# Strassen's seven block products for part of each second feed-forward matrix in a two-layer decoder trunk

## The chip, the cores and the metric

The kernel runs on one core of one Trainium2 chip. The metric is the device time of one execution in microseconds (us). Engines are named as in the profile: PE is TensorE (matmuls), PEld its weight loads, DVE is VectorE, ACT is ScalarE, POOL is GpSimd, SP is the engine whose queue starts the weight DMAs.

## The reference

The trunk works on 256 tokens of width 1024 and has two layers. Each layer is a feed-forward half step, a token mixer (a gated spatial unit and a differential attention side by side) and a second feed-forward half step, each followed by a layer norm over a scaled residual. There are four feed-forwards in all, and the change touches only them:

```python
def _swiglu(x, w1, w3, w2):
    return (jax.nn.silu(x @ w1) * (x @ w3)) @ w2
...
        h = _swiglu(x, ffn_w1[l, 0], ffn_w3[l, 0], ffn_w2[l, 0])
        x = _layernorm(ALPHA * x + 0.5 * h, ln_g[l, 0], ln_b[l, 0])
```

`w1` and `w3` are 1024 x 2816, `w2` is 2816 x 1024, all float32. The inner width 2816 is 22 k tiles of 128.

## The kernel before

**Number format.** Each float32 operand is split in two: a high part rounded to TensorE's fp32r type (ScalarE, a copy) and a low part, the difference (VectorE, a subtraction). A product is then three matmuls, high x high, low weight x high and high weight x low (`three`, matmuls at L208). For a weight piece of 1024 columns the high part is L166 and the low part L168, in `stream`; for activations they are L173 and L174, in `split`.

**Weights.** `stream` loads a piece of 1 MB (128 x 2048) into one of 4 `raw` buffers over SP's queue and splits it into two high and two low tiles of 1024 columns, out of 8 buffers each (`hi`, `lo`). A piece that is loaded early waits for these buffers, which come free when TensorE has used the tile. When the next stage's first weights would have to wait, some go to buffers of the activation pool instead (`lent`).

**A feed-forward** (`ffn`) has three parts. `gemm_b2` computes the first 4 of the 22 inner tiles with tokens as rows. Then `gemm_a2` runs nine times and makes two inner tiles each: 32 matmuls with the high weights over 512 columns (L220), 32 with the low weights over 256 columns (L227), an addition from PSUM (L230), silu on ScalarE (L523), a product on VectorE (L524) and the split of the result (L173, L174). Last comes the second matrix, in two calls of `gemm_b`, one for each 512 output columns: for each of 22 k tiles and each half of 128 tokens, three matmuls of 512 columns into one PSUM bank per token half. That is 264 matmuls (22 x 2 x 2 x 3) in a row. The last `tail` k tiles of a call are held back, so that token half 0 is finished ahead of token half 1: 4 k tiles in the first call, 14 in the second. In the last feed-forward of all, the block of token half 1 and column half 1 is computed in two banks of 256 columns.

`Norm.part` (L415, L419) adds a finished PSUM block to the scaled residual and takes its statistics, `Norm.finish` normalises a token half, `turned` transposes it on TensorE for the next stage.

**Order.** The order on TensorE is the order of the code. VectorE, ScalarE and the queues are ordered by a scheduler, from priorities that grow with each piece of weights (`step`). Each engine works its list strictly in that order. Pieces of work that are to lie beside the matmuls (`beside`, `beat`) are placed by counting matmul work.

Of the kernel before, what the change touches and what calls it, by code (L numbers as in the profile page):

```python
# [25 lines left out]
DFF = 2816  # L26
FT = DFF // P
FB = 4
HEADS = 8
HD = 64  # L30
GROUPS = 8
# [16 lines left out]


@with_exitstack  # L50
def trunk(ctx, tc, x, xT, w13a, w13b, w2, wb, wqk, wa, wbr, wo, gateb, sgug, sgub, sguwT, sgubias, lam, diffg,
          lng, lnb, lngT, lnbT, cosT, sinT, out):
    nc = tc.nc
    V, A, G, PE = nc.vector, nc.scalar, nc.gpsimd, nc.tensor
# [184 lines left out]
    def rows_b(ps, t, k0, piece, xh, xl, kts, c0=0, n=512):  # L239
# [6 lines left out]
                  k == 0, k == kts - 1)  # L246
        beat(n / 1024)

    def gemm_b(src, kts, xh, xl, done, tail=4, last=()):

        blocks = [[(bank(), c, n) for c, n in (last if t else ()) or ((0, 512),)] for t in range(NT)]
        held = []
        for c in range(0, kts, 4):
            nk = min(4, kts - c)
            for i, piece in enumerate(stream(src[:, c * 512 : (c + nk) * 512], nk * 512)):
                k = c + 2 * i
                if k >= kts - tail:
                    held.append((k, piece))
                    continue
                for t in range(NT):  # L260
                    for ps, o, n in blocks[t]:
                        rows_b(ps, t, k, piece, xh, xl, kts, o, n)
        for t in range(NT):
            for ps, o, n in blocks[t]:
                for k, piece in held:
                    rows_b(ps, t, k, piece, xh, xl, kts, o, n)
                done(t, ps[:, :n], o, n)

    def gemm_b2(srcs, xh, xl, done, norm=None):

# [115 lines left out]
    class Norm:  # L386
# [25 lines left out]
        def part(self, t, c, ps):  # L412
            s = slice(c, c + ps.shape[1])
            with behind(self.xlo.get((0, 0))):
                V.scalar_tensor_tensor(out=self.y[t][:, s], in0=self.y[t][:, s], scalar=self.scale, in1=ps,  # L415
                                       op0=ALU.mult, op1=ALU.add)
            for o in range(s.start, s.stop, self.group):
                g = o // self.group * 6
                V.bn_stats(out=self.st[t][:, g : g + 6], in_=self.y[t][:, o : o + self.group])  # L419
            if self.last and t == NT - 1 and s.stop < D:  # L420
                V.tensor_tensor(out=self.y[t][:, s], in0=self.y[t][:, s], in1=self.g[:, s], op=ALU.mult)
# [70 lines left out]

    def ffn(l, f, i, norm, last=False):
        xh, xl = parts(both)
        h_hi = [act.tile([P, 512], F32R, tag="slot", name=name("hhi")) for _ in range(FT // 2)]
        h_lo = [act.tile([P, 512], F32R, tag="slot", name=name("hlo")) for _ in range(FT // 2)]
        hh, hl = view(h_hi), view(h_lo)

        def front(t, ps):
            s = t512("silu")  # L500
# [4 lines left out]
        def turned(t, s):  # L505
            b = side_bank()
            for k in range(FB):
                PE.transpose(b[:, k * P : (k + 1) * P], s[:, k * P : (k + 1) * P], ident)  # L508
            b4 = b.rearrange("p (k t) -> p k t", k=4)
            for j in range(2):  # L510
                hi = h_hi[j].rearrange("p (k t) -> p k t", k=2)[:, :, t * P : (t + 1) * P]
                lo = h_lo[j].rearrange("p (k t) -> p k t", k=2)[:, :, t * P : (t + 1) * P]
                split(hi, lo, b4[:, 2 * j : 2 * j + 2])
            yield 0

# [4 lines left out]
        for j in range(FB, FT, 2):  # L520
            for m, z in gemm_a2([w13a[l, f, j - FB + m] for m in range(2)], both, lambda m: t512("silu")):
                s = z[:, :T]
                silu[0] = A.activation(s, s, AF.Silu).ins  # L523
                V.tensor_tensor(out=s, in0=s, in1=z[:, T:], op=ALU.mult)  # L524
                split(hh(j + m), hl(j + m), s)
# [5 lines left out]
        def done(t, p, c, n):  # L531
            ln.part(t, 512 + c, p)
            if c + n == 512:
                ln.finish(t, ((2, 1.5), (2, 1))[t])
# [227 lines left out]
    for l in range(DEPTH):  # L762
# [2 lines left out]
        norm = ffn(l, 1, 2, norm, last=l == DEPTH - 1)  # L765


_INS = ["x", "xT", "w13a", "w13b", "w2", "wb", "wqk", "wa", "wbr", "wo", "gateb", "sgug", "sgub", "sguwT", "sgubias",
        "lam", "diffg", "lng", "lnb", "lngT", "lnbT", "cosT", "sinT"]


def _layout(i):
# [34 lines left out]
    o["w2"] = halves(f["ffn_w2"])  # L807
# [40 lines left out]
```

## Time and profile before

| what | value |
|---|---|
| time, three runs | 1243.22, 1243.42 (median), 1244.21 us |
| span of the profiled execution | 1242.5 us, 0.9 us below the median of the runs; it has no other time of its own |
| TensorE busy | 1236.6 us (100% of the span) |
| VectorE busy | 873.1 us (70%) |
| ScalarE busy | 756.0 us (61%) |
| DMA | 241.87 MB, 195 GB/s in the mean |
| granted TensorE clock | 1.000 |

Busy shares are means over stages of different kinds. A row of a group gives the line, the engine, the operation, out<-in with the shape, the count, then the busy us with the mean ns of one, and the idle time just ahead of these instructions with what ended it. The first feed-forward's column groups run from 36 to 128.6 us, its second matrix to 188.5 us.

### The profile page before, as it was taken

What the parts mean: (1) busy time and instruction counts of PE and PEld (TensorE: products, weight loads), DVE (VectorE), ACT (ScalarE), POOL (GpSimd) and SP (SyncE); (2) the same over time, 40 slices, a digit from 0 to 9 for tenths busy, and PEclk for the clock granted to TensorE, in tenths of its full rate; (3) what the DMA queues carried; (4) which work ended last, traced back from release to release, by engine and by line L of the source; (5) the groups of instructions that cost most, each with busy time, mean ns of one, the idle gap of its engine ahead of it and who ended that gap; (6) DMA issues with size and microseconds to landing.
All of it is one profiled execution on the core that took longest, in us unless ns stands there. A gap on an engine that the chain in (4) does not pass through costs nothing.

```text
span 1242.5 us, 17870 instructions
## 1 busy us (share of the span) xinstructions
PE 1236.6 (100%) x6703; PEld 1064.1 (86%) x6703; DVE 873.1 (70%) x1532; ACT 756.0 (61%) x1388; POOL 86.0 (7%) x184
## 2 busy tenths in 40 slices
PE   9999999999999999999999999999999999999998
PEld 8888888888888888888888888888888888888887
DVE  6766567876587977665677665679756879766753
ACT  6776446679665566664466664466786555766640
POOL 0100000144100000000000000002430000000000
PEclk9999999999999999999999999999999999999999
DMA  9765645654754745556545546556556456455540
GB/s 352 276 204 183 224 171 187 227 167 165 248 183 145 244 162 205 177 180 253 194 169 191 192 159 250 203 184 206 162 175 228 165 174 233 170 203 203 165 174 35
DMA packets 40679, 241.87 MB, mean 195 GB/s; under 512 B 5344, under 2 KB 6416, under 8 KB 14480
## 3 DMA queue, kind: packets, MB, share of 16 engines
q1 hardware_dynamic: 36624, 227.82, 52.1%
q0 software_dynamic: 3536, 12.13, 3.0%
q8 instruction: 52, 0.85, 0.3%
q10 hardware_dynamic: 432, 0.79, 0.2%
q14 instruction: 35, 0.29, 0.1%
HBM read 235.47 MB, written 1.05 MB: 190 GB/s over the span
## 4 chain that ended last, share of the span: by engine, by line
PE 99%; DVE 0%; ACT 0%; issue 0%; DVEq 0%; ACTq 0%
PE bank L220 38%; PE bank L208 35%; PE bank L227 20%; PE bank L323 2%; PE sbank L588 1%; PE sbank L474 1%; PE sbank L637 1%; PE sbank L718 1%; PE sbank L335 0%; PE sbank L635 0%; PE sbank L659 0%; PE sbank L508 0%; PE sbank L622 0%; PE sbank L627 0%; PE sbank L446 0%; DVE xtok L454 0%
## 5 line engine op out<-in xcount | busy, mean ns | idle before, releaser
L168 DVE TENSOR_TENSOR wlo<-raw,whi 128x1024 fp32r<-128x1024 f32 (+1 forms) x442 | 490.0, 1127 | 223.4 <-PE bank L227 129.3
L166 ACT ACTIVATE whi<-raw 128x1024 fp32r<-128x1024 f32 (+1 forms) x442 | 425.8, 978 | 279.4 <-PE bank L208 135.3
L220 PE MATMUL bank<-x,whi 128*128 128x512 f32 x1792 | 426.5, 392 | 0.0
L220 PEld LDWEIGHTS bank<-x,whi 128*128 128x128 f32 x1792 | 330.7, 188 | 69.0 <-issue 2.6
L227 PE MATMUL bank<-x,wlo 128*128 128x256 f32 x1792 | 229.9, 284 | 0.0
L227 PEld LDWEIGHTS bank<-x,wlo 128*128 128x128 f32 x1792 | 224.2, 191 | 4.8
L208 PE MATMUL bank<-whi,hhi 128*128 128x512 f32 (+1 forms) x374 | 141.3, 378 | 0.0
L208 PE MATMUL bank<-wlo,hhi 128*128 128x512 f32 (+1 forms) x374 | 141.0, 377 | 0.0
L208 PE MATMUL bank<-whi,hlo 128*128 128x512 f32 (+1 forms) x374 | 140.9, 377 | 0.0
L228 ACT ACTIVATE r<-bank 128x256 f32<-128x256 f32 x256 | 96.5, 380 | 66.0 <-PE bank L227 65.7
L208 PE MATMUL bank<-whi,x 128*128 128x512 f32 x328 | 106.6, 394 | 0.0
L208 PEld LDWEIGHTS bank<-whi,hlo 128*128 128x128 f32 x374 | 70.4, 188 | 13.0
L208 PEld LDWEIGHTS bank<-wlo,hhi 128*128 128x128 f32 x374 | 70.4, 188 | 12.7
L208 PEld LDWEIGHTS bank<-whi,hhi 128*128 128x128 f32 x374 | 70.4, 188 | 12.7
L208 PEld LDWEIGHTS bank<-whi,x 128*128 128x128 f32 x328 | 61.6, 188 | 12.7
L208 PE MATMUL bank<-wlo,x 128*128 128x512 f32 x164 | 64.0, 390 | 0.0
L480 ACT ACTIVATE xf<-sbank,ln_b,ln_g 128x128 f32<-128x128 f32 x80 | 30.0, 456 | 40.2 <-PE sbank L474 40.2
L230 DVE TENSOR_TENSOR silu<-bank,r 128x256 f32<-128x256 f32 x144 | 54.2, 418 | 0.2
L383 POOL DMA_DIRECT2D bc<-in_lng x6 | 3.2, 530 | 727.7 <-DVE bc L382 727.7
L415 DVE SCALAR_TENSOR_TENSOR xtok<-xtok,bank 128x512 f32<-128x512 f32 (+1 forms) x25 | 16.6, 663 | 42.2 <-PE bank L208 42.2
L564 POOL TENSOR_TENSOR swap<-swap,sin_t 128x512 f32<-128x512 f32 x16 | 24.3, 1517 | 242.4 <-DMA swap<-z 226.7
L208 PE MATMUL bank<-lhi,x 128*128 128x512 f32 x120 | 39.9, 396 | 0.0
(183 smaller groups left out, 1254.1 us busy)
## 6 DMA issues: line engine op xcount, KB each, us to landing
raw<-in_w13a SPq DMA_DIRECT2D x72, 1024.0 KB, 5.0
raw<-in_w SPq DMA_DIRECT2D x40, 1024.0 KB, 4.9
raw<-in_wa SPq DMA_DIRECT2D x24, 1024.0 KB, 5.5
raw<-in_wb SPq DMA_DIRECT2D x16, 1024.0 KB, 4.9
raw<-in_wqk SPq DMA_DIRECT2D x16, 1024.0 KB, 5.1
raw<-in_wbr SPq DMA_DIRECT2D x16, 1024.0 KB, 4.9
raw<-in_w13b SPq DMA_DIRECT2D x12, 1024.0 KB, 5.0
raw<-in_wo SPq DMA_DIRECT2D x8, 1024.0 KB, 4.9
```

The source lines that it names most:

```text
L166: A.activation(h, r, AF.Copy)
L168: V.tensor_tensor(out=w, in0=r, in1=h.bitcast(F32), op=ALU.subtract)
L208: PE.matmul(ps, xx, w, start=start and n == 0, stop=stop and n == 2)
L220: PE.matmul(b[-1], hi[:, k * P : (k + 1) * P], xc(k), start=k == 0, stop=False)
L227: PE.matmul(b[n][:, :T], lo[:, k * P : (k + 1) * P], xc(k)[:, :T], start=False, stop=k == KT - 1)
L228: emptied[0] = A.activation(r[:, s], b[n][:, T:], AF.Copy, scale=scale).ins
L230: a = V.tensor_tensor(out=z[:, s], in0=b[n][:, :T], in1=r[:, s], op=ALU.add)
L323: PE.matmul(ps[t][m], x[:, j, o + t * P : o + (t + 1) * P], y, start=k0 + j == 0 and o == 0 and y is hi, stop=k0 + j == KT - 1 and y is lo)
L415: V.scalar_tensor_tensor(out=self.y[t][:, s], in0=self.y[t][:, s], scalar=self.scale, in1=ps, op0=ALU.mult, op1=ALU.add)
L474: PE.transpose(b[:, k * P : (k + 1) * P], self.y[t][:, h * 512 + k * P : h * 512 + (k + 1) * P], ident)
L480: A.activation(xf[:, s], b[:, s], AF.Identity, scale=self.gT[:, f], bias=self.bT[:, f])
L564: turned_by[0] = G.tensor_tensor(out=s3, in0=s3, in1=s, op=ALU.mult).ins
```

## The change

Of the 11 pairs of inner k tiles, six (`SQ`: tiles 4 and 5 up to 14 and 15) go through Strassen's seven products in the second matrix; five (`PQ`: 0 and 1, 2 and 3, 16 to 21) stay as they were. For a Strassen pair the 2 x 2 blocks are two token halves by two k tiles for the activations, and two k tiles by two column halves for the weights. The seven block products accumulate in seven PSUM banks `S[1]` to `S[7]`, over all six pairs.

- `mixed` makes the four sums of activation blocks on VectorE (L563 to L566) and splits the originals and the sums, 512 columns each (L177, L178), where two tiles of 256 were split.
- `stream_s` loads both column halves of a pair as one piece of 1 MB, splits three of the four blocks (`cut`, L294 on ScalarE and L296 on VectorE), makes three sums in place in `raw` on VectorE (L307, L309, L310) and splits the four results. Two pairs share one tile for their first block, so a pair takes three and a half tiles.
- After the sixth pair eight VectorE operations and one of ScalarE recombine the blocks into the residual (L464, L466, L622 to L626). `S[2]`, `S[3]` and `S[4]` stay open and become the sums of three of the four output blocks of the plain pairs.
- The plain pairs come last, with both column halves in one piece. The last four (`HELD`) are held back, so token half 0 ends 48 matmuls ahead of token half 1.
- The activation pool grows from 27 to 31 buffers; the ring of DMA descriptors that GpSimd writes is set to 8192 bytes.

The weights are only ordered otherwise in memory. Sums of weight blocks are made on the chip.

```diff
+NS = 6
+SQ = [(FB + 2 * p, FB + 2 * p + 1) for p in range(NS)]
+PQ = [(k, k + 1) for k in (0, 2, *range(FB + 2 * NS, FT, 2))]
+HELD = 4
...
-    act = ctx.enter_context(tc.tile_pool(name="act", bufs=27))
+    act = ctx.enter_context(tc.tile_pool(name="act", bufs=31))
...
+    def stream_s(src, pair):
+        step()
+        raw = raw_pool.tile([P, CH], F32, tag="raw", name=name("raw"))
+        nc.sync.dma_start(raw, src)
...
+        def cut(p, o, n):
+            h, w = (v[:, p[2] : p[2] + n] for v in p[:2])
+            r = raw[:, o : o + n]
+            with behind(latest[0]):
+                A.activation(h, r, AF.Copy)
+            with behind(latest[1]):
+                V.tensor_tensor(out=w, in0=r, in1=h.bitcast(F32), op=ALU.subtract)
...
+        b, c, d = ((*two(), 0) for _ in range(3))
+        cut(a, 0, 512)
+        cut(b, 1024, 1024)
+        V.tensor_tensor(out=raw[:, :1024], in0=raw[:, :1024], in1=raw[:, 512:1536], op=ALU.add)
+        cut(c, 0, 1024)
+        V.tensor_tensor(out=raw[:, 1024:1536], in0=raw[:, :512], in1=raw[:, 1024:1536], op=ALU.add)
+        V.tensor_tensor(out=raw[:, 1536:], in0=raw[:, 1024:1536], in1=raw[:, 1536:], op=ALU.add)
+        cut(d, 1024, 1024)
...
+        return keep, {1: at(a, 0), 3: at(b, 0), 2: at(b, 1), 5: at(c, 0), 7: at(c, 1), 6: at(d, 0), 4: at(d, 1)}
...
+        def mixed(q, qa):
+            qb = s512("qb")
+            a = qa.rearrange("p (k t) -> p k t", k=4)
+            V.tensor_tensor(out=qb[:, :T].rearrange("p (k t) -> p k t", k=2),
+                            in0=a[:, 1:2].to_broadcast([P, 2, P]), in1=a[:, ::3], op=ALU.subtract)
+            V.tensor_tensor(out=qb[:, T : T + P], in0=qb[:, P:T], in1=qa[:, :P], op=ALU.subtract)
+            V.tensor_tensor(out=qb[:, T + P :], in0=qa[:, T : T + P], in1=qb[:, T : T + P], op=ALU.add)
...
+            for j, v in enumerate((qa, qb)):
+                split(at[0][j], at[1][j], v)
...
-        gemm_b(w2[l, f, 0], FT, hh, hl, lambda t, p, c, n: ln.part(t, 0, p))
...
-        gemm_b(w2[l, f, 1], FT, hh, hl, done, tail=14, last=((0, 256), (256, 256)) if last else ())
+        S = {n: side_bank() for n in (3, 7, 4)}
+        S.update({n: bank() for n in (1, 2, 5, 6)})
+        pair = None
+        for n, q in enumerate(SQ):
+            pair, w = stream_s(w2s[l, f, n], pair)
+            for b in (3, 7, 4, 1, 2, 5, 6):
+                three(S[b], *s_op[q][b], *w[b], n == 0, n == NS - 1 and b in (1, 5, 6, 7))
+            beat(1.75)
+        u, v = s512("u"), s512("v")
+        A.activation(u, S[6], AF.Copy)
+        ln.more(1, 0, S[7], ALU.subtract, ln.scale)
+        ln.more(0, 0, S[1], ALU.add, ln.scale)
+        V.tensor_tensor(out=u, in0=u, in1=S[1], op=ALU.add)
+        V.tensor_tensor(out=v, in0=S[5], in1=u, op=ALU.subtract)
+        ln.more(0, 1, v, ALU.add, ln.scale)
+        ln.more(1, 1, v, ALU.add, ln.scale)
+        ln.more(1, 0, u, ALU.add)
+        ln.more(1, 1, S[7], ALU.add)
+        ends = {(0, 0): [(S[2], 0, 512)], (0, 1): [(S[3], 0, 512)], (1, 0): [(S[4], 0, 512)],
+                (1, 1): [(side_bank(), o, n) for o, n in (((0, 256), (256, 256)) if last else ((0, 512),))]}
+        held = []
+        for n, q in enumerate(PQ):
+            w = stream(w2p[l, f, n])
+            if n >= len(PQ) - HELD:
+                held.append((q, w))
+                continue
+            for c in range(2):
+                for t in range(NT):
+                    for ps, o, m in ends[t, c]:
+                        rows_p(ps, t, q, w[c], hh, hl, o, m, start=not n and t + c == 2)
+        for t in range(NT):
+            for c in range(2):
+                for ps, o, n in ends[t, c]:
+                    for q, w in held:
+                        rows_p(ps, t, q, w[c], hh, hl, o, n, stop=q == held[-1][0])
+                    ln.part(t, c * 512 + o, ps[:, :n], 1.0)
+            ln.finish(t, ((2, 1.5), (2, 1))[t])
...
-    nc = bacc.Bacc("TRN2", target_bir_lowering=False, num_devices=1)
+    nc = bacc.Bacc("TRN2", target_bir_lowering=False, num_devices=1, dynamic_dma_scratch_size=8192)
```

How VectorE's list changes is told by its order. First, VectorE at the end of the last column group of the first feed-forward, before the change; `wlo` is a low weight tile, `hlo` the low part of an activation:

```order
L168 TENSOR_TENSOR wlo_1471<-raw_1468,whi_1470 128x1024
L230 TENSOR_TENSOR silu_1337<-bank_1290,r_1336 128x256
L230 TENSOR_TENSOR silu_1337<-bank_1299,r_1336 128x256
L168 TENSOR_TENSOR wlo_1475<-raw_1468,whi_1474 128x1024
L524 TENSOR_TENSOR silu_1337<-silu_1337 128x256
L230 TENSOR_TENSOR silu_1363<-bank_1318,r_1362 128x256
L230 TENSOR_TENSOR silu_1363<-bank_1327,r_1362 128x256
L174 TENSOR_TENSOR hlo_166<-silu_1337,hhi_155 128x256
L524 TENSOR_TENSOR silu_1363<-silu_1363 128x256
```

The same place in the changed kernel; `slo` is a low tile of weight blocks, `raw_1487` the second Strassen pair:

```order
L296 TENSOR_TENSOR slo_1492<-raw_1487,shi_1491 128x1024
L608 TENSOR_TENSOR silu_1377<-silu_1377 128x256
L234 TENSOR_TENSOR silu_1403<-bank_1358,r_1402 128x256
L234 TENSOR_TENSOR silu_1403<-bank_1367,r_1402 128x256
L178 TENSOR_TENSOR hlo_154<-silu_1377,hhi_149 128x256
L608 TENSOR_TENSOR silu_1403<-silu_1403 128x256
L309 TENSOR_TENSOR raw_1487<-raw_1487 128x512
L178 TENSOR_TENSOR hlo_154<-silu_1403,hhi_149 128x256
L431 COPY bc_1430<-silu_1403 128x1
L431 COPY bc_1433<-silu_1403 128x1
L310 TENSOR_TENSOR raw_1487<-raw_1487 128x512
L296 TENSOR_TENSOR slo_1494<-raw_1487,shi_1493 128x1024
```

The splits of plain weights have become splits of the second pair's blocks, and two of its sums and its last split stand behind the silu work.

Second, VectorE in the middle of the Strassen pairs, where before only splits stood one behind the other. These are the third pair (`raw_1527`) and the fourth (`raw_1569`); two more splits of the third pair, of 512 and 1024 columns, stand just ahead:

```order
L307 TENSOR_TENSOR raw_1527<-raw_1527 128x1024
L296 TENSOR_TENSOR slo_1530<-raw_1569,shi_1529 128x512
L309 TENSOR_TENSOR raw_1527<-raw_1527 128x512
L296 TENSOR_TENSOR slo_1534<-raw_1527,shi_1533 128x1024
L310 TENSOR_TENSOR raw_1527<-raw_1527 128x512
L307 TENSOR_TENSOR raw_1569<-raw_1569 128x1024
L296 TENSOR_TENSOR slo_1536<-raw_1527,shi_1535 128x1024
L296 TENSOR_TENSOR slo_1572<-raw_1569,shi_1571 128x1024
L296 TENSOR_TENSOR slo_1574<-raw_1569,shi_1573 128x1024
L309 TENSOR_TENSOR raw_1569<-raw_1569 128x512
L310 TENSOR_TENSOR raw_1569<-raw_1569 128x512
L296 TENSOR_TENSOR slo_1576<-raw_1569,shi_1575 128x1024
```

The two pairs are worked in one another, fourteen operations in all; the last split stands straight behind the sum that it splits, and the fifth and sixth pair follow in the same pattern.

Third, VectorE behind the last pair. Ahead of these rows stand one L466, one L172, one L466 and two L172; `xtok` is the residual, `u` and `v` are the recombined blocks:

```order
L625 TENSOR_TENSOR u_1691<-u_1691,bank_1441 128x512
L172 TENSOR_TENSOR wlo_1744<-raw_1737,whi_1743 128x1024
L626 TENSOR_TENSOR v_1692<-bank_1443,u_1691 128x512
L464 TENSOR_TENSOR xtok_144<-xtok_144,u_1691 128x512
L466 SCALAR_TENSOR_TENSOR xtok_143<-xtok_143,v_1692 128x512
L466 SCALAR_TENSOR_TENSOR xtok_144<-xtok_144,v_1692 128x512
L172 TENSOR_TENSOR wlo_1750<-raw_1747,whi_1749 128x1024
L464 TENSOR_TENSOR xtok_144<-xtok_144,sbank_1439 128x512
L172 TENSOR_TENSOR wlo_1754<-raw_1747,whi_1753 128x1024
L172 TENSOR_TENSOR wlo_1760<-raw_1757,whi_1759 128x1024
L172 TENSOR_TENSOR wlo_1764<-raw_1757,whi_1763 128x1024
L172 TENSOR_TENSOR wlo_1770<-raw_1767,whi_1769 128x1024
```

The recombination stands between the splits of the plain pairs; the last row is the first column half of the last held pair.

More of the change, by code (lines that the diff above doesn't have):

```diff
@@ L247, in rows_b, with rows_p @@
         beat(n / 1024)
+    def rows_p(ps, t, q, piece, xh, xl, c0=0, n=512, stop=False, start=False):
+        for j, k in enumerate(q):
+            wh, wl = (v[:, j * 512 + c0 : j * 512 + c0 + n] for v in piece)
+            three(ps[:, :n], xh(k)[:, t * P : (t + 1) * P], xl(k)[:, t * P : (t + 1) * P], wh, wl,
+                  start and j == 0, stop and j == 1)
+        beat(n / 1024)
     def gemm_b(src, kts, xh, xl, done, tail=4, last=()):
@@ L410, in __init__, with more, part @@
                 self.x = [xs.tile([P, 4, 512], F32R, tag="x", name=name("x")) for _ in range(2)]
-        def part(self, t, c, ps):
+        def more(self, t, c, v, op, scale=1.0):
+            y = self.y[t][:, c * 512 : (c + 1) * 512]
+            if scale == 1.0:
+                V.tensor_tensor(out=y, in0=y, in1=v, op=op)
+            else:
+                V.scalar_tensor_tensor(out=y, in0=y, scalar=scale, in1=v, op0=ALU.mult, op1=op)
+        def part(self, t, c, ps, scale=None):
             s = slice(c, c + ps.shape[1])
+            y = self.y[t][:, s]
             with behind(self.xlo.get((0, 0))):
-                V.scalar_tensor_tensor(out=self.y[t][:, s], in0=self.y[t][:, s], scalar=self.scale, in1=ps,
-                                       op0=ALU.mult, op1=ALU.add)
+                if scale == 1.0:
+                    V.tensor_tensor(out=y, in0=y, in1=ps, op=ALU.add)
+                else:
+                    V.scalar_tensor_tensor(out=y, in0=y, scalar=self.scale, in1=ps, op0=ALU.mult, op1=ALU.add)
             for o in range(s.start, s.stop, self.group):
@@ L806, in _layout, with blocks @@
     o["w13b"] = c(np.concatenate([halves(w1[..., :nb]), halves(w3[..., :nb])], axis=2))
-    o["w2"] = halves(f["ffn_w2"])
+    w2 = f["ffn_w2"].reshape(L, 2, FT, P, 2, 512)
+    def blocks(at):
+        return c(np.stack([w2[:, :, k, :, h] for k, h in at], axis=3)).reshape(L, 2, P, CH)
+    o["w2s"] = c(np.stack([blocks(((a, 0), (a, 1), (b, 1), (b, 0))) for a, b in SQ], axis=2))
+    o["w2p"] = c(np.stack([blocks(((a, 0), (b, 0), (a, 1), (b, 1))) for a, b in PQ], axis=2))
     u, v, q, k, val, ga, gb = (f["w_in"][:, :, s * D : (s + 1) * D] for s in range(7))
```

47 lines of the change are left out of this document (34 added, 13 removed).

## The prediction

> **What bounds the kernel now.** I read the page's busy shares and its chain of waits first, to see which engine sets the end.
>
> ```profile
> PE 1236.6 (100%) x6703; PEld 1064.1 (86%) x6703; DVE 873.1 (70%) x1532; ACT 756.0 (61%) x1388; POOL 86.0 (7%) x184
> PE 99%; DVE 0%; ACT 0%; issue 0%; DVEq 0%; ACTq 0%
> ```
>
> TensorE (PE) is busy all of the span and is 99% of the chain that ended last. So a matmul taken out saves its step, as long as nobody makes TensorE wait. VectorE (DVE) has 30% idle in the mean, but the mean covers several stages. I therefore took the stage table next: the w1/w3 columns of the first feed-forward (35 to 128 us) and its second matrix (128.4 to 188.6 us).
>
> ```profile
> core 0: us, PE busy (x) PEld busy (x) DVE busy (x) ACT busy (x) POOL busy (x), PEclk, DMA share, GB/s
> 35.00:128.00 93.00, 93.00 (x547) 82.72 (x546) 64.14 (x120) 63.56 (x109) 4.96 (x9) 1.00 0.61 206
> 128.40:188.60 60.20, 60.20 (x270) 49.87 (x270) 36.11 (x55) 27.36 (x39) 1.06 (x2) 1.00 0.59 215
> ```
>
> In the second-matrix stage VectorE works 36.1 of 60.2 us. The change puts its new VectorE work into the first half of exactly this stage. The steps of TensorE come from the chain in order of time.
>
> ```profile
> 117.62 7.28 PE bank L220 x32
> 124.90 3.83 PE bank L227 x32
> 128.73 57.15 PE bank L208 x252
> 1174.14 60.83 PE bank L208 x330
> ```
>
> A 512-column matmul takes 57.15 / 252 = 0.2268 us, a 256-column one 3.83 / 32 = 0.1197 us. A second-matrix stage of 264 matmuls is 59.9 us, from 128.6 to 188.5 us. In the last feed-forward, where one block is split into halves, it is 198 x 0.2268 + 132 x 0.1197 = 60.7 us, which the last row (60.83) confirms.
>
> VectorE's steps come from its own instructions in order of time; the second column is a duration, or for several the length of the run.
>
> ```profile
> 183.78 3.70 DVE L168 TENSOR_TENSOR wlo<-raw,whi 128x512 fp32r<-128x512 f32 x6
> 189.16 0.68 DVE L415 SCALAR_TENSOR_TENSOR xtok<-xtok,bank 128x512 f32<-128x512 f32 x1
> 189.88 0.69 DVE L419 BATCH_NORM_STATS2 st<-xtok 128x6 f32<-128x512 f32 x1
> 212.00 3.49 DVE L168 TENSOR_TENSOR wlo<-raw,whi 128x1024 fp32r<-128x1024 f32 x3
> ```
>
> The step from start to start is (3.49 - 1.22) / 2 = 1.135 us for 1024 columns, and (3.70 - 0.69) / 5 = 0.602 us for 512. Where an instruction needs the result of the one ahead of it, its start comes 0.72 us later instead of 0.60 (189.16 to 189.88), so a dependence costs 0.12.
>
> **The change part by part.** *Taken out on TensorE.* A pair of k tiles needs 24 matmuls before (2 k, 2 token halves, 2 column halves, 3 products) and 21 after (7 blocks, 3 products). Six pairs save 18 of 264 per feed-forward: 54 x 0.2268 = 12.25 us in the first three. In the last, 198 full and 132 half-width matmuls become 216 and 60: 72 x 0.1197 - 18 x 0.2268 = 4.54 us. Together 16.8 us, if nothing waits.
>
> *Added on VectorE, per pair.* The seven blocks are 3584 columns to split where the pair had 2048, and three sums come on top. The prices:
>
> ```profile
> L168 DVE TENSOR_TENSOR wlo<-raw,whi 128x1024 fp32r<-128x1024 f32 x360 | 436.7, 1227 | 213.1 <-PE bank L227 126.8 <-ACT whi L166 70.7 <-issue 15.2
> L465 DVE TENSOR_TENSOR xtok<-xtok,bc 128x1024 f32<-128x1024 f32 x20 | 24.1, 1220 | 0.0
> L166 ACT ACTIVATE whi<-raw 128x1024 fp32r<-128x1024 f32 x360 | 378.2, 1059 | 225.8 <-PE bank L220 125.8 <-PE bank L208 91.5 <-ACT hhi L173 3.1
> ```
>
> An in-place sum of 1024 columns (L465, 1220 ns) costs what a split does (1227 ns), so sums and splits share the steps above. A pair is one 512 and three 1024 splits, one 1024 and two 512 sums: 4 x 1.135 + 3 x 0.602 = 6.35 us. TensorE eats a pair in 21 x 0.2268 = 4.76 us. So in this stage **VectorE becomes the bound**, unless it has run far enough ahead.
>
> *How far ahead it can run.* A pair takes three and a half of the eight lo buffers, so two pairs fit and half of a first tile more. Even those can't be done early, because the last w1/w3 columns hold four lo buffers until TensorE's last matmuls of L227. The rows of before show that wait at this place, and what follows:
>
> ```profile
> 125.89 1.22 DVE L168 TENSOR_TENSOR wlo<-raw,whi 128x1024 fp32r<-128x1024 f32 x1 [3.81 <-PE bank L227]
> 127.03 0.75 DVE L230 TENSOR_TENSOR silu<-bank,r 128x256 f32<-128x256 f32 x2
> 127.69 1.22 DVE L168 TENSOR_TENSOR wlo<-raw,whi 128x1024 fp32r<-128x1024 f32 x1
> 128.83 0.42 DVE L524 TENSOR_TENSOR silu<-silu 128x256 f32<-128x256 f32 x1
> 131.96 0.22 DVE L382 COPY bc<-silu 128x1 f32<-128x1 f32 x2
> 132.09 2.36 DVE L168 TENSOR_TENSOR wlo<-raw,whi 128x1024 fp32r<-128x1024 f32 x2
> 134.24 1.06 ACT L166 ACTIVATE whi<-raw 128x1024 fp32r<-128x1024 f32 x1 [1.66 <-PE bank L208]
> 135.33 1.23 DVE L168 TENSOR_TENSOR wlo<-raw,whi 128x1024 fp32r<-128x1024 f32 x1 [0.88 <-ACT whi L166]
> ```
>
> In the changed order the splits at 125.89 and 127.69 are blocks 3, 2 and 5, 7 of the *second* pair, with the same two adds between. So when TensorE starts the stage (128.6), VectorE stands at 128.83 with the first pair done and two sums and a split of the second still to come. I carry the changed order down from there.
>
> 1. *Rest of the second pair.* Five 256-column operations of the silu stage (0.33 each, from the pair of 0.75 at 127.03), a 512 sum, one more 256, the two copies (0.13), the last sum in full (0.69): 132.2 us. The next split needs ScalarE's copy of that sum: 0.03 + 1.06 + 0.03 (the 0.03 from 135.30 to 135.33 in the last two rows), then 1.135: 134.5 us.
> 2. *Pairs three and four, then five and six.* The scheduler interleaves two pairs. Eight 1024 and six 512 operations: 9.08 + 3.61 = 12.7 us. Three waits come on top: 0.12 between the two dependent sums, 0.09 for a copy of ScalarE that a 1024 sum almost covers, and 1.21 at the end, where the last split waits for ScalarE with nothing placed in between. That is 14.1 us against TensorE's 9.53. Twice: 162.7 us.
> 3. *Plain pairs and the recombination.* Up to the first column half of the last held pair stand nine splits and eight 512 operations that add the Strassen blocks into the residual: 9 x 1.135 + 8 x 0.602 = 15.0, so that split ends at 177.8 us. TensorE has 5.44 us for the first plain pair and 3 x 1.36 us for three held ones from about 165.9, and so stands before it from 175.5, with two waits.
> 4. *Rest on TensorE.* 126 + 24 + 18 + 1 matmuls are done then, 77 are left: 17.5 us, end at 195.4.
>
> The stage ends 6.9 us later than before (188.5), in three feed-forwards; in the last, 66.8 us and 48 half-width matmuls for 24 full ones (+0.30) stand against 60.8: +6.3. The **sum is +27.0 us**: 44 us of new waits less 16.8 saved. On the span that gives 1242.5 + 27.0 = 1269.5; the runs' median lies 0.9 us above the span, and I take as much around it after: **1270 us**.
>
> The Trainium skill, "VectorE: DVE Perf Modes" (The DRAIN you can't avoid), says that the next VectorE operation does not start until the pipe has emptied. By that rule a step would be the full 1.22 and 0.69 us, step 2 would be 15.3 and step 3 16.6 us, and the sum +43 us. The trace disagrees: six of 0.69 us take 3.70.
>
> *At no cost.* The activation sums and the wider splits of a pair (one 256, two 128-wide sums, and two 512 splits for two of 256: about 1.5 us) fall into the 11.11 us (7.28 + 3.83) of two column groups. VectorE works 64.14 / 93.00 of that, 7.7 us, so they fit with 1.9 us to spare; without that cover they would be some 9 us per feed-forward. The weights stay 11 pieces of 1 MB on the same queue, at 215 GB/s, and a raw buffer is held no longer than VectorE is behind. [...] At the end of the stage the first token half's norm has 48 matmuls (10.9 us) of cover, where it had 42 (9.5), so the turn to the next stage costs nothing new.
>
> *Bounds.* Below: VectorE hides all waits of steps 1 and 2, about 1.1 + 2 x 1.42 us, 16 us over four: 1254. Above: each operation at its full duration, 4 us more per feed-forward: 1287. I stay near my sum, since every operation has a row of its own kind.
>
> **The rivals.** *Hidden after all, faster.* If VectorE gave two pairs within 9.53 us, or entered the stage with about 11 us more done, only the 16.8 us would count: 1226.6. For it speaks the idle 29 us of VectorE between 35 and 128; against it the row at 125.89, where that idle is a wait for buffers, and 6.35 against 4.76.
>
> *A smaller loss.* The waits of steps 1 and 2 overlap better than the order lets me see: 1254 to 1260. Against it stands the wait at 135.33, which shows such a wait on ScalarE in full.
>
> *TensorE's clock falls.* With waits of around 1.2 us every few matmuls, the granted clock, 1.00 in both stage rows, might halve in the stage. Then 84 matmuls for pairs three to six would take 38.1 us instead of VectorE's 28.2: about +10 us per feed-forward, 1310. No row of before shows the clock below 1.00, and no wait I count reaches 1.4 us. The Trainium skill, "TensorE: Matmul & The Clock Gate" (A second HAM failure mode: psum-queue depth-cycling), says that frequent short idles between groups made the clock oscillate in one kernel; nothing in this trace can show it.
>
> *VectorE slower than its rows*, since sums and splits follow each other without a break: the upper bound, 1287.
>
> **How the numbers follow.** My sum 0.76, smaller loss 0.09, VectorE slower 0.05, clock 0.03, hidden 0.05, a wash 0.02. A measurement here tells about 0.2% (2.5 us) from no change, so faster is 0.05, same 0.02, slower 0.93. The range 1257 to 1284 takes in my sum with 14 us to either side, most of both bounds, and leaves out the ends.
>
> **What would show it.** The page after should have TensorE busy about 1220 us of a span near 1270, VectorE about 1040 (873 plus 42 per feed-forward), and the chain should have VectorE's splits and sums in it, four times some 36 us. In the stage, pairs three to six should take 14.1 us per two on TensorE, with waits of about 1 us for L296, and two more before the held pairs. The clock should be 1.00. Wrong would be my step 2 if two pairs come within 12 us, my step 3 if no wait stands before the held pairs, and everything if VectorE shows idle time in the stage for buffers while TensorE is full.

## The result and the profile after

The changed kernel takes 1275.15 us (median of four runs, 1273.26 to 1278.46) against 1243.58 us for the kernel before (four runs, 1243.22 to 1244.21). The ratio is 1.0256, with an interval from 1.0241 to 1.0272. Its profiled execution took 1274.34 us, with a span of 1272.6 us. That is 30.1 us more span than before, where 27.0 had been forecast. Of the executions reported below one, of the kernel with four pairs in a row, took 1738.84 us at a granted clock of 0.655, and that kernel's time is the median of its three others.

The page of the changed kernel: busy time of the engines, the granted clock in 40 slices, and the chain of waits by engine and by line.

```profile
PE 1240.9 (98%) x6595; PEld 1055.6 (83%) x6595; DVE 1028.5 (81%) x1756; ACT 797.1 (63%) x1440; POOL 86.2 (7%) x184
...
PEclk9999899999999999998999998999999999999989
...
PE 82%; DVE 13%; issue 3%; ACT 2%; DVEq 0%; ACTq 0%
PE bank L224 35%; PE bank L231 18%; PE bank L212 17%; PE sbank L212 6%; DVE slo L296 5%; PE bank L372 2%; DVE wlo L172 2%; ACT shi L294 2%; DVE raw L307 2%; DVE raw L310 1%; PE sbank L701 1%; DVE raw L309 1%; PE sbank L533 1%; DVE xtok L466 1%; PE sbank L750 1%
```

TensorE issues 108 matmuls fewer, as the change says, and yet its busy time is 4 us higher. VectorE's busy time rose by 155 us. Three things are new against the page of before: the chain, 99% TensorE then, now holds VectorE at 13%, with its splits (L296, L172), its sums (L307, L309, L310) and its recombination (L466); ScalarE's copies (L294) are in it; and the clock has slices below full.

The same weight piece late in the w1/w3 columns tells how the extra time is spread. The chain of the kernel before has these three rows (start, length, the matmuls of one column group):

```profile
458.57 7.26 PE bank L220 x32
...
643.13 7.26 PE bank L220 x32
...
1073.71 7.26 PE bank L220 x32
```

and the chain of the changed kernel the same three:

```profile
467.00 7.26 PE bank L224 x32
...
659.71 7.26 PE bank L224 x32
...
1097.06 7.26 PE bank L224 x32
```

They are 8.43, 16.58 and 23.35 us later, and the end is 30.1 us later. The loss per feed-forward with what follows it is therefore 8.4, 8.2, 6.8 and 6.8 us, where 6.9 (three times) and 6.3 had been forecast. It arises in the four second-matrix stages; the first of them shows how. Its windows in the changed kernel:

```profile
core 0: us, PE busy (x) PEld busy (x) DVE busy (x) ACT busy (x) POOL busy (x), PEclk, DMA share, GB/s
128.40:137.90 9.50, 9.50 (x43) 7.84 (x43) 8.37 (x17) 5.25 (x9) 1.06 (x2) 1.00 0.58 232
137.90:152.30 14.40, 11.83 (x44) 8.80 (x43) 13.09 (x15) 7.10 (x9) 0.00 (x0) 0.88 0.47 168
152.30:166.60 14.30, 11.91 (x37) 8.51 (x37) 11.40 (x13) 8.83 (x10) 0.00 (x0) 0.76 0.42 140
```

In the first 9.5 us, pairs one and two, TensorE runs full with 43 matmuls. In the next two stretches it gets through 44 and 37 in over 14 us each, while VectorE is busy 13.1 and 11.4 us of them. DMA moves less (168 and 140 GB/s, for 232). That alone could also mean late weights; but in the last two stretches VectorE waits only for ScalarE and TensorE, and ScalarE only for VectorE and TensorE. In order of time, VectorE's instructions there (start, length, and in brackets the idle time before with its releaser):

```profile
133.08 2.96 DVE L296 TENSOR_TENSOR slo<-raw,shi 128x1024 fp32r<-128x1024 f32 x3 [1.13 <-ACT shi L294]
...
147.42 2.96 DVE L296 TENSOR_TENSOR slo<-raw,shi 128x1024 fp32r<-128x1024 f32 x3 [1.21 <-ACT shi L294]
...
161.79 1.23 DVE L296 TENSOR_TENSOR slo<-raw,shi 128x1024 fp32r<-128x1024 f32 x1 [1.20 <-ACT shi L294]
164.60 0.69 DVE L466 SCALAR_TENSOR_TENSOR xtok<-xtok,sbank 128x512 f32<-128x512 f32 x1 [1.58 <-PE sbank L212]
...
175.07 5.76 DVE L172 TENSOR_TENSOR wlo<-raw,whi 128x1024 fp32r<-128x1024 f32 x5
```

From the last split of the second pair to that of the fourth are 147.42 - 133.08 = 14.34 us, and to that of the sixth 161.79 - 147.42 = 14.37 us. Each ends in the wait for ScalarE of 1.2 us. The 14.35 us are 4.8 more than the 9.53 that TensorE needs for two pairs: 12.7 us of VectorE's own steps make 3.2 of it, its waits the other 1.6. Then comes something new: the first recombination (L466) stands at the head of VectorE's queue and waits 1.58 us for TensorE. TensorE over the same time:

```profile
139.64 0.50 PE L212 MATMUL sbank<-slo,shh 128*128 128x512 f32 x1 [0.77 <-DVE slo L296]
...
141.41 0.50 PE L212 MATMUL sbank<-shi,shh 128*128 128x512 f32 x1 [1.04 <-ACT shi L294]
...
142.68 0.79 PE L212 MATMUL sbank<-slo,shh 128*128 128x512 f32 x1 [0.76 <-DVE slo L296]
143.27 0.63 PE L212 MATMUL sbank<-shi,shl 128*128 128x512 f32 x1
143.69 0.63 PE L212 MATMUL bank<-shi,shh 128*128 128x512 f32 x1
...
177.48 0.50 PE L212 MATMUL bank<-wlo,hhi 128*128 128x512 f32 x1 [1.10 <-DVE wlo L172]
...
179.75 0.50 PE L212 MATMUL bank<-wlo,hhi 128*128 128x512 f32 x1 [0.61 <-DVE wlo L172]
```

It waits for VectorE's splits and ScalarE's copies by turns, and before the held pairs twice more for splits. Behind the third wait the matmuls follow each other at 143.69 - 143.27 = 0.42 us where a step is 0.2268: the clock is at half. The view of all waits, summed over the execution (total us, how many, the longest), has TensorE's in these rows:

```profile
PE sbank L212 <- DVE slo L296: 11.6, 16, 0.8
PE sbank L212 <- ACT shi L294: 7.6, 8, 1.0
PE bank L212 <- DVE wlo L172: 4.9, 6, 1.1
PE sbank L212 <- DVE xtok L464: 2.2, 1, 2.2
```

That is 26 us of visible waiting, where the loss against full use is 30.1 + 16.8 = 47 us. The rest counts as busy: a matmul's end is shown 0.39 us behind its start although the next could follow after 0.2268, so each wait hides some 0.16 us of itself, and at half clock a waiting engine looks like a working one. For 31 waits the first comes to 5 us, and a mean clock of 0.988 over 1272.6 us hides another 15; with the 26 us that is nearly all of the 47. This is why the busy time of TensorE didn't fall.

### The profile page after: what moved, and what is told of

Its sections match the earlier page's. It is cut to its first block, busy times and chain, and to the rows that moved or that the text cites. A ratio compares the mean times of both kernels' runs of the same rounds, so it can differ in the third digit from the quotient of the medians.

```text
span 1272.6 us, 18004 instructions
## 1 busy us (share of the span) xinstructions
PE 1240.9 (98%) x6595; PEld 1055.6 (83%) x6595; DVE 1028.5 (81%) x1756; ACT 797.1 (63%) x1440; POOL 86.2 (7%) x184
## 4 chain that ended last, share of the span: by engine, by line
PE 82%; DVE 13%; issue 3%; ACT 2%; DVEq 0%; ACTq 0%
PE bank L224 35%; PE bank L231 18%; PE bank L212 17%; PE sbank L212 6%; DVE slo L296 5%; PE bank L372 2%; DVE wlo L172 2%; ACT shi L294 2%; DVE raw L307 2%; DVE raw L310 1%; PE sbank L701 1%; DVE raw L309 1%; PE sbank L533 1%; DVE xtok L466 1%; PE sbank L750 1%
## 5 line engine op out<-in xcount | busy, mean ns | idle before, releaser
L172 DVE TENSOR_TENSOR wlo<-raw,whi 128x1024 fp32r<-128x1024 f32 (+1 forms) x394 | 432.8, 1113 | 89.2 <-PE bank L231 46.9
L170 ACT ACTIVATE whi<-raw 128x1024 fp32r<-128x1024 f32 (+1 forms) x394 | 372.0, 966 | 179.1 <-PE bank L224 114.6
L294 ACT ACTIVATE shi<-raw 128x1024 fp32r<-128x1024 f32 (+1 forms) x96 | 86.2, 945 | 75.8 <-DVE raw L310 49.0
L296 DVE TENSOR_TENSOR slo<-raw,shi 128x1024 fp32r<-128x1024 f32 (+1 forms) x96 | 101.7, 1087 | 29.6 <-PE bank L231 15.3
L212 PE MATMUL sbank<-whi,hhi 128*128 128x512 f32 (+1 forms) x130 | 48.9, 376 | 2.2 <-DVE xtok L464 2.2
L212 PE MATMUL sbank<-whi,hlo 128*128 128x512 f32 (+1 forms) x130 | 48.5, 373 | 0.0
L212 PE MATMUL sbank<-wlo,hhi 128*128 128x512 f32 (+1 forms) x130 | 48.5, 373 | 0.0
L711 ACT ACTIVATE pp<-pp,mx 128x256 f32<-128x256 f32 (+1 forms) x64 | 28.3, 443 | 12.8 <-DVE mx L709 12.8
L178 DVE TENSOR_TENSOR x<-xf,x 128x512 fp32r<-128x512 f32 x20 | 13.8, 689 | 27.8 <-ACT x L177 27.8
```

The lines of the kernel that those rows point to most:

```text
L170: A.activation(h, r, AF.Copy)
L172: V.tensor_tensor(out=w, in0=r, in1=h.bitcast(F32), op=ALU.subtract)
L212: PE.matmul(ps, xx, w, start=start and n == 0, stop=stop and n == 2)
L294: A.activation(h, r, AF.Copy)
L296: V.tensor_tensor(out=w, in0=r, in1=h.bitcast(F32), op=ALU.subtract)
L711: A.activation(p[:, s], p[:, s], AF.Exp, bias=mx[:, a], scale=-1.0, accum_out=sums[:, a])
```

## The experiments

The theory (A, where a text gives letters) is the prediction's: VectorE can't prepare Strassen pairs as fast as TensorE eats them, and the pairs come one behind the other. The rivals are that the fallen clock takes most of the time, and that the weights come late. The medians of the kernel before were 1243.89 us beside the first four runs and 1243.49 us beside the last three.

**Without the three sums.** The weight blocks are split as they are loaded, so the output is that of other block products; TensorE's work is the same.

```diff
-        V.tensor_tensor(out=raw[:, :1024], in0=raw[:, :1024], in1=raw[:, 512:1536], op=ALU.add)
...
-        V.tensor_tensor(out=raw[:, 1024:1536], in0=raw[:, :512], in1=raw[:, 1024:1536], op=ALU.add)
-        V.tensor_tensor(out=raw[:, 1536:], in0=raw[:, 1024:1536], in1=raw[:, 1536:], op=ALU.add)
```

> The three in-place sums of weight blocks (L307, L309, L310) are left out, so the seven products are formed from unsummed blocks and the result is not the reference's; matmuls, splits and loads are the changed kernel's. Theory A (VectorE's rate binds): a pair costs VectorE 0.602 + 3 x 1.135 = 4.0 us, less than TensorE's 4.76, so TensorE's waits in the stage go away but for the recombination's, and the saved matmuls show: 1227 to 1232 us, granted clock 1.00. Rival B (the seven-bank order on TensorE, the recombination or the held plain pairs cost the time): 1255 us or more, with waits left on TensorE before the held pairs.

Measured: 1232.2 us (1231.19 to 1233.89), ratio 0.9909 (0.9894 to 0.9924). The page's busy times, and the one wait of TensorE in a second-matrix stage:

```profile
PE 1219.7 (99%) x6595; PEld 1048.5 (85%) x6595; DVE 970.8 (79%) x1684; ACT 797.7 (65%) x1440; POOL 86.2 (7%) x184
...
PE sbank L212 <- DVE xtok L461: 4.1, 1, 4.1
```

With 72 VectorE instructions fewer, and not one matmul fewer, 43 us are gone and the kernel is faster than before. VectorE's mean share hardly moved (81% to 79%). The waits for splits and copies have all gone, and so has the half clock (mean 0.999). So what TensorE saves is real, and what is lost hangs on VectorE's and ScalarE's preparation of the pairs: late weights and slower block products are out. The 4.1 us are a wait of the last feed-forward, which comes up again below.

**The clock held up.** Sixteen small matmuls into a spare bank go ahead of blocks 7 and 4 of the third and fifth pair, where TensorE would stand idle.

```diff
+            if n == 0:
+                idle = side_bank()
             for b in (3, 7, 4, 1, 2, 5, 6):
+                if n in (2, 4) and b in (7, 4):
+                    for _ in range(16):
+                        PE.matmul(idle[:, :P], warm, warm, start=True, stop=True)
```

> 16 matmuls of 128 columns on a constant tile, into an unused bank, stand ahead of blocks 7 and 4 of the third and fifth Strassen pair, so that TensorE does not stand idle where it waits for VectorE. Theory A: VectorE sets the pace and the fallen clock is a consequence; it costs only where the sixth pair ends late and the first recombination operation waits 1.58 us for it. With the clock near 1.00, 4 x 1.6 us come back at most: 1268 to 1273 us, VectorE's splits of the fifth pair at the same times as now. Rival C (the fallen clock is a main cause: half speed in the 3.0 and 5.5 us stretches of the stage, about 4.2 us of matmul time lost per feed-forward): 17 us come back, 1258 us.

Measured: 1273.6 us (1273.51 to 1273.69), ratio 1.0240 (1.0223 to 1.0258), just above the range expected. The windows of pairs three to six, and VectorE behind them, in this kernel:

```profile
137.90:152.30 14.40, 12.75 (x76) 9.40 (x74) 13.09 (x15) 7.09 (x9) 0.00 (x0) 1.00 0.46 161
152.30:166.60 14.30, 12.65 (x75) 9.53 (x75) 12.98 (x15) 9.20 (x11) 0.00 (x0) 1.00 0.43 145
```

```profile
161.46 1.23 DVE L296 TENSOR_TENSOR slo<-raw,shi 128x1024 fp32r<-128x1024 f32 x1 [1.21 <-ACT shi L294]
162.60 0.68 DVE L466 SCALAR_TENSOR_TENSOR xtok<-xtok,sbank 128x512 f32<-128x512 f32 x1
...
173.07 5.76 DVE L172 TENSOR_TENSOR wlo<-raw,whi 128x1024 fp32r<-128x1024 f32 x5
```

The clock is back at 1.00, the 1.58 us of L466 are gone, and the pairs take as long as with the fallen clock: the last split of the sixth pair starts at 161.46 instead of 161.79, and the stage itself starts 0.36 us earlier (127.85, for 128.21). VectorE sets their pace. From the first second-matrix matmul to the first matmul of the next stage the changed kernel took 70.0, 68.9 and 68.3 us in the first three feed-forwards; here it is 68.3 in each. So the clock cost 1.7, 0.6 and 0 us there. Of these 2.3 us the last feed-forward gave 1.5 back here, since the clock fell in it behind a wait of 2.2 us (0.50 for 3.41 us; the last section shows these rows). The clock is a consequence of the waits, and it costs little.

**Four pairs, between plain ones.** Four Strassen pairs instead of six, each followed by a plain pair while there is one; then the recombination and four held pairs. The last block of the last feed-forward is one bank of 512 columns.

```diff
-NS = 6
+NS = 4
...
-        for n, q in enumerate(SQ):
-            pair, w = stream_s(w2s[l, f, n], pair)
...
+        for kind in "SPSPSPS":
+            if kind == "S":
+                q = SQ[n]
+                pair, w = stream_s(w2s[l, f, n], pair)
...
+            else:
+                w = stream(w2p[l, f, p])
+                for c in range(2):
+                    for t in range(NT):
+                        for ps, o, m in ends[t, c]:
+                            rows_p(ps, t, PQ[p], w[c], hh, hl, o, m, start=not p and t + c == 2)
+                p += 1
```

> Four Strassen pairs instead of six, with one plain pair between each two of them (S P S P S P S), then four held plain pairs as now; the last block of the last feed-forward is one bank of 512 columns. Theory A: a Strassen and a plain pair cost VectorE 6.35 + 2.27 = 8.6 us and TensorE 4.76 + 5.44 = 10.2 us, so VectorE keeps up; 48 matmuls saved are 10.9 us and the joined halves 0.8 us: 1232 us, faster than before by 0.9%, clock 1.00. Rival B (Strassen's banks and recombination cost time whatever the order): 1243 us or more.

Measured: 1230.77 us (1230.67 to 1231.27), ratio 0.9897 (0.9882 to 0.9911). It beats both kernels. Busy times and two windows:

```profile
PE 1223.1 (100%) x6589; PEld 1050.4 (85%) x6589; DVE 981.8 (80%) x1692; ACT 781.1 (64%) x1424; POOL 85.7 (7%) x184
```

```profile
128.40:150.00 21.60, 21.60 (x97) 17.87 (x96) 20.28 (x27) 12.35 (x16) 1.06 (x2) 1.00 0.67 241
150.00:170.00 20.00, 20.00 (x90) 16.57 (x89) 17.52 (x21) 12.53 (x16) 0.00 (x0) 1.00 0.84 301
```

TensorE is full in both, at full clock, with VectorE at 94% and 88%. By the counts this kernel saves 3 x 12 x 0.2268 = 8.2 us and in the last feed-forward 60.7 - 252 x 0.2268 = 3.5; it gained 13.1. The other 1.4 us aren't accounted for in full: the first second-matrix stage starts at 127.72 instead of 128.57, so 0.85 of them lie ahead of the second matrix.

**The same four in a row.** One word differs from the paced kernel.

```diff
-        for kind in "SPSPSPS":
+        for kind in "SSSSPPP":
```

> The same four Strassen pairs and the same total work on every engine as with S P S P S P S, but the four one behind the other, then three plain pairs, then the held ones. Theory A: pairs three and four take VectorE 14.1 us against 9.5, so each feed-forward is late by about 4.2 us where the paced order is not: 1232 + 17 = 1249 us, 1 to 4 us more if the clock falls in the waits. Theory A' (what binds is VectorE's total, not its rate in one place): the same time as the paced order within 3 us.

Measured: 1254.21 us (1254.01 to 1254.51), ratio 1.0085 (1.0068 to 1.0101). Busy times, and the window that held pairs three and four:

```profile
PE 1236.5 (99%) x6589; PEld 1057.0 (84%) x6589; DVE 982.1 (78%) x1692; ACT 783.4 (63%) x1424; POOL 87.1 (7%) x184
```

```profile
137.90:152.30 14.40, 11.64 (x37) 8.51 (x36) 12.81 (x14) 8.63 (x9) 0.00 (x0) 0.76 0.44 146
```

The instruction counts of TensorE and VectorE, and VectorE's busy time, are those of the paced kernel, and the end is 23.4 us later. So it isn't how much work VectorE has, but in which stretch it falls. It came 5 us above the 1249 expected, of which up to 4 had been allowed for the clock. The next kernel takes that apart.

**Four in a row, clock held up.** The kernel with four in a row gets two groups of sixteen small matmuls per feed-forward.

```diff
+                    if n == 2 and b in (7, 4):
+                        for _ in range(16):
+                            PE.matmul(ends[1, 1][0][0][:, :P], warm, warm, start=True, stop=True)
```

> Four pairs one behind the other, with 16 matmuls of 128 columns on a constant tile ahead of blocks 7 and 4 of the third pair, in a bank that is not yet in use; VectorE's list is the same. With four in a row and no filling the second matrix's stage took 6.3 us more than in the paced order (64.3 against 58.0), where VectorE's rate alone gave 4.2. If the rest is the fallen clock (13 matmuls at half speed, 2.6 us, behind the third pair), the clock stays at 1.00 and the stage comes to 62 us: 1245 to 1247 us. If the rest has another cause, it stays at 1253 to 1255.

Measured: 1250.91 us (1250.41 to 1251.56), ratio 1.0060 (1.0045 to 1.0075). This lies between the two answers that had been expected, so both theories were off in size. The window and VectorE's last split of the fourth pair:

```profile
137.90:152.30 14.40, 12.46 (x75) 9.29 (x74) 12.81 (x14) 9.07 (x11) 0.00 (x0) 1.00 0.43 151
```

```profile
147.55 1.23 DVE L296 TENSOR_TENSOR slo<-raw,shi 128x1024 fp32r<-128x1024 f32 x1 [1.21 <-ACT shi L294]
```

The clock cost 1254.21 - 1250.91 = 3.3 us, 0.8 per feed-forward. The other 1250.91 - 1230.77 = 20.1 us, 5.0 per feed-forward, I put down to VectorE; I had said 4.2. Two pairs in 14.35 us instead of 9.53 would be 4.8. The last split, which TensorE needs for the end of its fourth pair, starts at 147.55; with all operands in time TensorE would have been through with that pair at 128.05 + 84 x 0.2268 = 147.1, and it ended at 152.15.

**Without the recombination.** The ten lines that turn the seven blocks into the residual are left out, so the output lacks the four Strassen sums.

```diff
-        u, v = s512("u"), s512("v")
-        A.activation(u, S[6], AF.Copy)
-        ln.more(1, 0, S[7], ALU.subtract, ln.scale)
...
-        ln.more(1, 1, S[7], ALU.add)
```

> The changed kernel without the recombination (eight VectorE operations and one ScalarE copy per feed-forward), so that products 1, 5, 6 and 7 never reach the result and it is not the reference's. By step 3 of the prediction the waits before the held pairs stem from these 8 x 0.602 us and from the wait of the first of them: nine splits alone end at about 173 us, ahead of TensorE's 175.5, so both waits go and 2 to 4 us per feed-forward come back: 1259 to 1267 us. If the waits before the held pairs stem from late loads (ScalarE waited 1.83 us there for a piece of weights), the time stays at 1272 to 1278.

Measured: 1264.91 us (1264.18 to 1269.85), ratio 1.0180 (1.0161 to 1.0200). VectorE's plain splits behind the sixth pair:

```profile
162.94 9.16 DVE L172 TENSOR_TENSOR wlo<-raw,whi 128x1024 fp32r<-128x1024 f32 x8
172.84 2.36 DVE L172 TENSOR_TENSOR wlo<-raw,whi 128x1024 fp32r<-128x1024 f32 x2 [0.74 <-ACT whi L170]
```

The splits now follow at once and no wait stands before the held pairs; 10 us are back, 2.5 per feed-forward. So the waits before the held pairs come from VectorE's list (splits with the recombination among them). Plain weights loaded late are not the cause, although ScalarE does wait for the last of them in the changed kernel:

```profile
173.28 2.01 ACT L170 ACTIVATE whi<-raw 128x1024 fp32r<-128x1024 f32 x2 [1.83 <-DMA raw<-in_w2p]
```

The first of these two copies, 1.06 us long, is done by 174.34, and VectorE gets to its split only at 175.07 + 3 x 1.135 = 178.5.

**One sum doubled.** The 1024-column sum of each pair is done twice, so that the blocks made from it hold one term twice; VectorE has one step of 1.135 us per pair more, TensorE nothing.

```diff
         V.tensor_tensor(out=raw[:, :1024], in0=raw[:, :1024], in1=raw[:, 512:1536], op=ALU.add)
+        V.tensor_tensor(out=raw[:, :1024], in0=raw[:, :1024], in1=raw[:, 512:1536], op=ALU.add)
```

> The 1024-column sum of weight blocks (L307) stands twice in each pair, so the blocks are wrong and the result is not the reference's. If VectorE's rate sets the pace of pairs three to six, each of them gains one step and a dependence, 1.135 + 0.12 = 1.26 us, 5.0 us per feed-forward, and part of the second pair's besides: 1295 to 1302 us. If TensorE's own waits (clock, banks) set the pace, the time rises by less than 8 us.

Measured: 1304.25 us (1303.62 to 1305.94), ratio 1.0492 (1.0474 to 1.0509), 2 us above the range expected. VectorE's last splits of pairs four and six:

```profile
151.25 2.96 DVE L296 TENSOR_TENSOR slo<-raw,shi 128x1024 fp32r<-128x1024 f32 x3 [1.21 <-ACT shi L294]
...
167.79 1.23 DVE L296 TENSOR_TENSOR slo<-raw,shi 128x1024 fp32r<-128x1024 f32 x1 [1.20 <-ACT shi L294]
```

Two pairs take 167.79 - 151.25 = 16.54 us instead of 14.37: 2.17 more, nearly the two steps of 1.135 (2.27). The 29.1 us over the changed kernel are 7.3 per feed-forward: 4.3 from pairs three to six, 1.6 from the second pair (its last split stood at 133.08, now at 134.70), and 1.4 that I put down to the lower clock (0.977) without having separated them. In pairs three to six VectorE's added work passes to the end nearly one for one, as it must where VectorE sets the pace. The four stages don't share the loss evenly: from the first second-matrix matmul to the next stage the first three grew by 5.9, 6.5 and 8.1 us.

## Why the prediction was right, and where it was off

1270 us was forecast, 1275.15 measured, inside the range. The mechanism, VectorE as the bound of the stage, is shown from four sides: taking its sums away, doubling one, and taking its recombination away each moved the time with the changed kernel's matmuls, and spacing the pairs moved it against the same four pairs in a row.

- *Taken out on TensorE, 16.8 us.* Borne out as far as it can be seen: without the sums the time fell 11.7 us below that of before with one wait of 4.1 us left in it.
- *Step 1*, the second pair: its last split starts at 133.08 and takes a step of 1.135, so 134.2 where 134.5 had been forecast.
- *Step 2*, 14.1 us for two pairs: 14.34 and 14.37. The end of the sixth pair's last split, forecast for 162.7, came at 161.79 + 1.135 = 162.9.
- *Step 3* is the step that failed in size. Its work was right: nine splits and eight recombination operations were put at 15.0 us, and from 164.60 to the end of the ninth split (175.07 + 3 x 1.135 + 1.22 = 179.7) they take 15.1. But I let them start when the splits of step 2 end. The first of them isn't a split, it is the recombination of block 7, which needs the last matmul of that block from the sixth pair, and TensorE was late with it at half clock: 1.58 us at the head of the queue, and the splits behind it waited too. With the clock held up the ninth split ends at 173.07 + 3 x 1.135 + 1.22 = 177.7, and 177.8 was the forecast.
- *Step 4*, 77 matmuls: the two waits before the held pairs are there (1.10 and 0.61), in three feed-forwards. In the last one they aren't; in their place stands one wait of 2.2 us that I didn't see coming. There the last block has two half banks, and the second of them is the bank of block 7, which comes free only when the recombination has read it (L464). In the kernel without sums it is 4.1 us, since TensorE is there earlier.
- *The sum*: 6.9, 6.9, 6.9 and 6.3 us forecast, 8.4, 8.2, 6.8 and 6.8 measured. Of the 3.1 us between them the clock's part of the first two feed-forwards is 1.7 + 0.6 = 2.3 us, by the kernel with the clock held up. The rest, 0.8, I can't divide further. Part of the closeness is luck. From its first matmul to the next stage's first, each of these stages took 60.36 us before, and the first three take 70.0, 68.9 and 68.3 now, so they lose 9.7, 8.5 and 7.9. The stretches behind them came out 0.9, 0.4 and 1.2 us shorter, 0.36 us of each because four transposes now stand ahead of that next matmul instead of behind it; the prediction had nothing for this.
- *At no cost* holds for the activation sums: TensorE's first second-matrix matmul starts at 128.21, where it started at 128.57. No run varies the activation pool or the descriptor ring alone; the paced kernel has both and is faster than the kernel before.
- *The clock at 1.00* was wrong: the mean is 0.988, and in the stage it stands at 0.50 for some microseconds. As a rival I had set its price at 10 us per feed-forward, with the half clock for all of pairs three to six. It lasts only for a part of them, and TensorE, which waits for VectorE anyway, catches up; the price was 0 to 1.7. A matmul at half clock took 0.427 us besides (4.27 us for ten steps from 158.06 on), so even 84 of them are 35.9 us and not 38.1.
- *TensorE busy about 1220* was wrong for the reason given with the waits: 1240.9. VectorE's 1028.5 stands near the 1040 forecast, which had added too much: 24.5 us for six pairs, 9 for the activations and 4.8 for the recombination are 38.3 per feed-forward and not 42, and 38.9 came.
- *The rivals*: hidden after all (1226.6) is nearly what the kernel without sums shows, 1232.2, so its condition, and not its price, failed. The smaller loss falls with 14.35 us for two pairs, and VectorE at its rows' full durations falls with the same number: that bound was 15.3.

## What to carry to other kernels

An engine with 30% idle in the mean can still be the bound of a stage: set what it needs per piece there (6.35 us for a pair) against what the next engine takes for it (4.76), and count how many pieces ahead the buffers let it run. Where the rate is short, put a light piece between two heavy ones before giving the idea up: the same four pairs cost 1254.2 us in a row and 1230.8 us between plain ones. And for each place where an engine's list turns from one kind of work to another, ask what the first instruction waits for, since all behind it waits too.

## What the hardware showed that I had not expected

The granted clock halves although TensorE never stands idle for long. In the changed kernel it fell to 0.50 at 142.29, in the last of three waits of 0.77, 1.04 and 0.76 us that end between 139.64 and 142.68. The Trainium skill, "TensorE: Matmul & The Clock Gate" (A second HAM failure mode: psum-queue depth-cycling), tells of frequent short idles between groups of matmuls that made the clock swing in one kernel; this trace agrees, with no wait over 1.04 us. It isn't the length of a wait alone that decides. The same wait of 2.2 us in the last feed-forward left the clock at 1.00 in the changed kernel (it ended at 1242.35) and was followed by 0.50 in the kernel with the fillers (it ended at 1240.03).

The traces show what goes with it. In every profile here the moments at which the clock changes lie a multiple of 3.41 us apart (142.29, 145.71, 155.95 and 162.78 in the first stage of the changed kernel). Cut at these moments, the rows give TensorE's busy time and the clock of each stretch:

```profile
138.88:142.29 3.41, 1.23 (x3) 0.48 (x3) 3.34 (x4) 1.99 (x3) 0.00 (x0) 1.00 0.11 48
142.29:145.71 3.42, 3.03 (x7) 2.46 (x8) 3.38 (x5) 0.97 (x2) 0.00 (x0) 0.50 0.60 187
...
152.53:155.95 3.42, 1.61 (x6) 0.68 (x5) 3.35 (x5) 1.45 (x3) 0.00 (x0) 1.00 0.07 29
155.95:159.36 3.41, 2.82 (x7) 1.85 (x8) 3.41 (x4) 1.67 (x2) 0.00 (x0) 0.50 0.38 79
159.36:162.78 3.42, 3.42 (x10) 2.65 (x9) 2.18 (x3) 2.08 (x3) 0.00 (x0) 0.50 0.54 228
...
1237.97:1241.39 3.42, 2.16 (x13) 1.72 (x11) 3.42 (x6) 1.91 (x2) 0.00 (x0) 1.00 0.42 177
1241.39:1244.80 3.41, 2.45 (x14) 2.17 (x15) 3.41 (x5) 1.06 (x1) 0.00 (x0) 1.00 0.02 5
```

and in the kernel with the fillers:

```profile
1236.43:1239.84 3.41, 1.40 (x10) 1.08 (x8) 3.41 (x6) 1.14 (x2) 0.00 (x0) 1.00 0.22 94
1239.84:1243.25 3.41, 3.22 (x11) 2.84 (x12) 3.41 (x4) 1.06 (x1) 0.00 (x0) 0.50 0.02 5
```

The clock of a stretch goes with the busy time of the stretch before it. At full clock 1.23, 1.40 and 1.61 us of 3.41 were followed by half clock, 2.16 and 2.45 were not. At half clock 2.82 left it at half, and 3.03, 3.22 and 3.42 were followed by full clock. The wait of 2.2 us lies across two stretches in the changed kernel and almost whole in one with the fillers, which is the difference between them. Over all nine profiles, at full clock every stretch with less than 1.5 us busy was followed by half clock and none with more than 1.9, and those between went both ways; at half clock up to 2.93 us left it at half, and 2.95 and more brought it back. No run shifted a wait against these moments to test it. Sixteen small matmuls in a wait kept the clock at 1.00 in pairs three to six of all four stages.
